# Strided attention on one core: own semaphores, whole-block casts in turn, and two streams that begin at a 128-instruction border

## The chip, the cores and the metric

The kernel runs on one core of a Trainium2 chip. The metric is device time in microseconds; three runs of the kernel before took 129.59, 129.45 and 129.51 us, median 129.51.

The core has five engines with an instruction stream each: PE (TensorE, matrix products), DVE (VectorE), ACT (ScalarE), POOL (GpSimd) and SP (SyncE, which here issues all transfers). Sixteen DMA engines move data between HBM and SBUF.

## The reference

Q, K and V are 8 x 12 x 1024 x 64 in float32. Every query attends to 16 keys, those at positions 0, 64, 128, ... of its head:

```python
attend_positions = np.arange(0, seq, stride)          # stride 64: 16 positions
q, k, v = Q[:, :, i:i+1, :], K[:, :, attend_positions, :], V[:, :, attend_positions, :]
scores  = einsum('bhqd,bhkd->bhqk', q, k) / sqrt(dim)
weights = exp(scores - max(scores)); weights /= sum(weights) + 1e-10
result[:, :, i, :] = einsum('bhqk,bhkd->bhqd', weights, v)
```

All of Q (25 MB) is read and as much output is written; of K and V only 0.4 MB each is needed.

## The kernel before

The 96 heads are worked on in 24 blocks of four heads (`g`, 0 to 23); a block has 1 MB of queries and 1 MB of output. Each block goes through these steps, named by function:

- `load(g)`: SP issues one transfer of the block's queries into one of ten float32 buffers `qn`.
- `cast(g)`: float32 to bf16 into `qb` (two buffers), the first half on POOL (L200) and the second on ACT (L201), 1,024 columns each.
- `transpose(g)`: DVE transposes 32 x 32 tiles of 32-bit pairs into `qt` (L205, two buffers).
- `scores(g)`: PE makes the scores with four matrix products from `k_t` and `qt` (L212); ACT takes the exponential of each half into `w` (L223).
- `values(g)`: POOL spreads the block's value rows over a mask into `v` (L191, three buffers). Four columns more of `v` hold a selector, so that the product also gives the sums of the weights.
- `outputs(g, c)`, c = 0, 1, 2: PE multiplies `w` by `v` for 3, 2 and 3 query groups (L237, two PSUM buffers in turn); DVE takes the reciprocal of the sums (L245); for c = 0 and 1 DVE multiplies into `out_sb` (L247), for c = 2 ACT copies the sums out of PSUM (L249) and POOL multiplies in place (L250).
- `store(g)`: SP issues one transfer of `out_sb` (eight buffers) to HBM.

Ahead of the loop POOL builds an identity matrix and from it `perm_v` with eight copies (L118), POOL and DVE clear `k_t` and the `w` buffers (L123, L127, L129), and DVE builds the selector `s_sel` from two iotas in three steps (L132 to L139), three copies of it and a mask. `key_rows` and `keys` lay out the keys in thirds: the first ahead of the loop, the others within blocks 1 to 3 and 5 to 7; `value_rows` does the values in halves, the second within block 4.

The order of work on every engine is the order in which the code records it (`manual_schedule`). In round `g` the code records `transpose(g + 2)`, `scores(g + 1)`, `values(g + 2)`, `cast(g + 3)`, then the three `outputs` of block g, then `store(g)` and `load(g + 10)`. Buffers come from rotating pools, and the framework places the semaphores and the waits. Its transfers go round eight semaphores, so that each transfer waits until the eighth one before it has landed.

Of the kernel before, what the change touches and what calls it, by code (L numbers as in the profile page):

```python
# [11 lines left out]
FP32 = mybir.dt.float32  # L12
BF16 = mybir.dt.bfloat16
# [29 lines left out]

@with_exitstack  # L50
def kernel(
# [24 lines left out]
    const = ctx.enter_context(tc.tile_pool(name="const", bufs=1))  # L76
    qn_pool = ctx.enter_context(tc.tile_pool(name="qn", bufs=QBUFS))
    out_pool = ctx.enter_context(tc.tile_pool(name="outsb", bufs=OBUFS))
    qb_pool = ctx.enter_context(tc.tile_pool(name="qb", bufs=2))
    qt_pool = ctx.enter_context(tc.tile_pool(name="qt", bufs=2))  # L80
    rec_pool = ctx.enter_context(tc.tile_pool(name="rec", bufs=2))
    psum_sc = ctx.enter_context(tc.tile_pool(name="psc", bufs=2, space=bass.MemoryType.PSUM))
    psum_o = ctx.enter_context(tc.tile_pool(name="po", bufs=2, space=bass.MemoryType.PSUM))

    ctx.enter_context(tc.manual_schedule())


    k_raw = const.tile([P, NC, D], FP32, name="k_raw")
    v_raw = const.tile([P, NC, D], FP32, name="v_raw")
    kv_src = [[stride * D, P], [2 * HG * SD, NC], [1, D]]  # L90
    qn = {}

    def load(g):
        qn[g] = qn_pool.tile([P, 32 * D], FP32, name="qn", tag="qn")
        n = P if g < 2 else 32
        _copy(nc, qn[g], _ap_with(Q, [[HG * SD // n, n], [1, HG * SD // n]], g * HG * SD))

    nc.sync.dma_start(k_raw, _ap_with(K, kv_src))
    load(0)
    nc.sync.dma_start(v_raw, _ap_with(V, kv_src))  # L100
# [3 lines left out]

    identity = const.tile([P, P], BF16, name="identity")
    make_identity(nc, identity)
    id_v = identity.rearrange("p (c b a k) -> p c b a k", c=2, b=2, a=2)

    perm_v = const.tile([P, 2, 2, 2, 2, NK], BF16, name="perm_v")

    iota_p = const.tile([P, 1], I16, name="iota_p")
    nc.gpsimd.iota(iota_p, pattern=[[0, 1]], base=0, channel_multiplier=1)
    col4 = const.tile([P, 4], I16, name="col4")
    nc.gpsimd.iota(col4, pattern=[[1, 4]], base=0, channel_multiplier=0)
    for c in range(2):
        for a in range(2):
            for e in range(2):
                nc.gpsimd.tensor_copy(  # L118
                    out=perm_v[:, c, a, :, e], in_=id_v[:, c, :, a]
                )  # L120

    k_t = const.tile([P, NG, 2, KW], BF16, name="k_t")
    nc.vector.memset(k_t[:, 0:8], 0.0)  # L123
    w_bufs = []
    for i in range(3):
        w = const.tile([P, 8, P], BF16, name=f"w{i}")
        nc.vector.memset(w, 0.0)  # L127
        w_bufs.append(w)
    nc.gpsimd.memset(k_t[:, 8:NG], 0.0)  # L129

    slot_i = const.tile([P, 1], I16, name="slot_i")
    nc.vector.tensor_scalar(  # L132
        out=slot_i, in0=iota_p, scalar1=4, scalar2=3,
        op0=ALU.logical_shift_right, op1=ALU.bitwise_and,
    )
    slot_f = const.tile([P, 1], FP32, name="slot_f")
    nc.vector.tensor_copy(out=slot_f, in_=slot_i)
    s_sel = const.tile([P, 4], BF16, name="s_sel")
    nc.vector.tensor_scalar(  # L139
        out=s_sel, in0=col4, scalar1=slot_f, scalar2=None, op0=ALU.is_equal  # L140
    )
    v_bufs = []
    for i in range(3):
        v = const.tile([P, 4 * D + 4], BF16, name=f"v{i}")
        nc.vector.tensor_copy(out=v[:, 4 * D :], in_=s_sel)
        v_bufs.append(v)
    mask = const.tile([P, 4, D], BF16, name="mask")
    nc.vector.tensor_copy(out=mask, in_=s_sel.unsqueeze(2).to_broadcast([P, 4, D]))

    k_bf = const.tile([P, NC, D], BF16, name="k_bf")  # L150
    k_r = const.tile([P, NC, D], BF16, name="k_r")
    v_bf = const.tile([P, NC, D], BF16, name="v_bf")
    v_rep = const.tile([P, NC, 2, D], BF16, name="v_rep")


    def key_rows(m):
        part = slice(4 * m, 4 * m + 4)
        nc.scalar.copy(k_bf[:, part], k_raw[:, part])  # L158
        nc.vector.transpose(  # L159
            k_r[:, part].rearrange("p n d -> p (n d)").bitcast(I32),  # L160
            k_bf[:, part].rearrange("p n d -> p (n d)").bitcast(I32),
        )


    def keys(m, c):
        for s in range(4):
            src, dst, col = 32 * (2 * c + s % 2), 32 * (2 * (s % 2) + s // 2), NK + 32 * s
            op = nc.vector.tensor_copy if m == 0 and s >= 2 else nc.scalar.copy
            op(  # L169
                k_t[dst : dst + 32, 8 * m + c : 8 * m + 8 : 2, :, col : col + NK],  # L170
                k_r[src : src + 32, 4 * m : 4 * m + 4].rearrange(
                    "p n (a k f) -> p a n f k", a=2, f=2
                )[:, s // 2],
            )


    def value_rows(n):
        for c in range(2):
            vp = psum_sc.tile([P, NC // 2, D], FP32, name="vp", tag="sc")
            nc.tensor.matmul(  # L180
                vp, lhsT=perm_v[:, c].rearrange("p a b e k -> p (a b e k)"),
                rhs=v_bf[:, 6 * n : 6 * n + 6], start=True, stop=True,
            )
            nc.vector.tensor_copy(out=v_rep[:, 6 * n : 6 * n + 6, c], in_=vp)  # L184

    qb, qt, wt, vb, rec, out_sb = {}, {}, {}, {}, {}, {}


    def values(g):
        vb[g] = v_bufs[g % 3]  # L190
        nc.gpsimd.tensor_tensor(  # L191
            out=vb[g][:, 0 : 4 * D].rearrange("p (s d) -> p s d", s=4), in0=mask,
            in1=v_rep[:, g // 2, g % 2].unsqueeze(1).to_broadcast([P, 4, D]),
            op=ALU.mult,
        )

    def cast(g):
        qb[g] = qb_pool.tile([P, 32 * D], BF16, name="qb", tag="qb")
        half = 16 * D
        nc.gpsimd.tensor_copy(out=qb[g][:, 0:half], in_=qn[g][:, 0:half])  # L200
        nc.scalar.copy(qb[g][:, half:], qn[g][:, half:])  # L201

    def transpose(g):
        qt[g] = qt_pool.tile([P, 32 * D], BF16, name="qt", tag="qt")
        nc.vector.transpose(qt[g].bitcast(I32), qb[g].bitcast(I32))  # L205

    def scores(g):
        sc = psum_sc.tile([P, 512], FP32, name="sc", tag="sc")
        q = qt[g]
        for e in range(2):  # L210
            for f in range(2):
                nc.tensor.matmul(  # L212
                    sc, lhsT=k_t[:, g, f, NK * (1 - e) : NK * (1 - e) + P],
                    rhs=_ap_with(
                        q, [q.ap[0], [D, 8], [16 * D, 2], [2, 32]],
                        extra_offset=8 * D * e + f,
                    ),
                    start=e + f == 0, stop=e + f == 2,
                )
        w = wt[g] = w_bufs[g % 3]  # L220
        for a in range(2):
            wa = w[64 * a : 64 * a + 64]
            nc.scalar.activation(  # L223
                out=_ap_with(wa, [wa.ap[0], [P, 8], [1, 2], [2, 32]], extra_offset=64 * a),
                in_=sc[64 * a : 64 * a + 64].rearrange("p (t x q) -> p t x q", t=8, x=2),
                func=AF.Exp, bias=0.0, scale=scale,
            )


    def outputs(g, c):  # L230
        if c == 0:
            out_sb[g] = out_pool.tile([P, 4, 8, D], FP32, name="out_sb", tag="out_sb")
            rec[g] = rec_pool.tile([P, 8, 4], FP32, name="rec", tag="rec")
        i0, n = ((0, 3), (3, 2), (5, 3))[c]
        ps = psum_o.tile([P, 3, 512], FP32, name="o_ps", tag="o")
        for i in range(n):
            nc.tensor.matmul(  # L237
                ps[:, i, 0 : 4 * D + 4], lhsT=wt[g][:, i0 + i], rhs=vb[g],
                start=True, stop=True,
            )  # L240
        r = rec[g][:, i0 : i0 + n]
        o = ps[:, 0:n, 0 : 4 * D].rearrange("p i (s d) -> p i s d", s=4)
        to = out_sb[g][:, :, i0 : i0 + n].rearrange("p s i d -> p i s d")
        by = r.unsqueeze(3).to_broadcast([P, n, 4, D])
        nc.vector.reciprocal(r, ps[:, 0:n, 4 * D : 4 * D + 4])  # L245
        if c < 2:
            nc.vector.tensor_tensor(out=to, in0=o, in1=by, op=ALU.mult)  # L247
        else:
            nc.scalar.copy(to, o)  # L249
            nc.gpsimd.tensor_tensor(out=to, in0=to, in1=by, op=ALU.mult)  # L250

    def store(g):
        o = out_sb[g]
        _copy(
# [3 lines left out]
        )  # L258
# [8 lines left out]
    nc.vector.tensor_copy(out=v_bf, in_=v_raw)  # L267
# [16 lines left out]
    for g in range(NG):  # L284
# [13 lines left out]
        if g + QBUFS < NG:  # L298
            load(g + QBUFS)
# [33 lines left out]
```

## Time and profile before

| What | Value |
|---|---|
| median of three runs | 129.51 us (129.45 to 129.59) |
| profiled execution: span | 127.7 us (the page gives no other time of it) |
| median less that span | 1.8 us |
| busy share of the span | DVE 69%, ACT 67%, POOL 63%, PE 50% |
| data queue (q1) | 51.12 MB, 96.7% of 16 DMA engines |
| mean rate | 401 GB/s over the span |
| HBM | 25.95 MB read, 25.17 MB written |

The span runs from the first to the last instruction of the profiled execution. Idle time of an engine in the page is put down to whatever ended it. The DMA share of a stretch is the mean over the 16 DMA engines of the time that their packets took, so it can pass 1 a little where packets overlap. The granted clock is the share of full speed at which PE ran; it was 0.858 over the span.

### The profile page before, as it was taken

The page shows a single profiled execution, that of the slowest core. Times are in us where ns is not written, and L with a number is a line of the kernel's source. Part 1 is how long each engine was busy: PE and PEld are TensorE (multiplying, and loading weights), DVE is VectorE, ACT ScalarE, POOL GpSimd, SP SyncE. Part 2 cuts the span into 40 slices and gives each one's busy share as a digit, 9 for nine tenths or more (in the row PEclk, how much of TensorE's full clock was granted, in tenths as well). Part 3 has the DMA queues.
Part 4 walks back from the last instruction along what each step waited for, and adds up shares of the span by engine and source line. Part 5 has one row for each costly group of instructions (what it writes and reads, how often), then busy time and mean ns, then how long its engine had stood idle before and what let it go on. Part 6 is the DMA issues. An engine that isn't in the chain of part 4 may idle for free.

```text
span 127.7 us, 1234 instructions
## 1 busy us (share of the span) xinstructions
PE 63.5 (50%) x292; PEld 29.8 (23%) x292; DVE 88.5 (69%) x167; ACT 86.1 (67%) x120; POOL 80.1 (63%) x89
## 2 busy tenths in 40 slices
PE   0006559256756628653696646366777646410000
PEld 0002223123322313332243313133423313200000
DVE  6956691869698696859769799797987976720000
ACT  4161917886999968999958979979787885320000
POOL 8933709554875876577866997969689694450000
PEclk9999999996799986999559999999856999955555
DMA  2999989998997998989989999999999999999980
GB/s 66 379 320 467 472 349 482 380 452 354 467 482 326 498 413 369 495 362 421 493 357 431 470 380 444 434 403 462 428 393 449 398 428 418 428 426 421 431 352 36
DMA packets 7911, 51.20 MB, mean 401 GB/s; under 512 B 3872, under 2 KB 3872, under 8 KB 3872
## 3 DMA queue, kind: packets, MB, share of 16 engines
q1 hardware_dynamic: 7904, 51.12, 96.7%
q8 instruction: 2, 0.03, 0.1%
q14 instruction: 5, 0.04, 0.1%
HBM read 25.95 MB, written 25.17 MB: 400 GB/s over the span
## 4 chain that ended last, share of the span: by engine, by line
POOL 37%; issue 33%; DVE 10%; PE 6%; ACT 2%; POOLq 1%; DVEq 0%
POOL qb L200 15%; POOL out_sb L250 12%; POOL v L191 10%; PE sc L212 4%; DVE out_sb L247 3%; PE o_ps L237 2%; DVE s_sel L139 2%; POOLq L328 1%; DVE w L127 1%; DVE qt L205 1%; ACT qb L201 1%; DVE rec L245 1%; DVE k_t L123 1%; ACT out_sb L249 1%; ACT k_t L169 0%
## 5 line engine op out<-in xcount | busy, mean ns | idle before, releaser
L237 PE MATMUL o_ps<-v,w 128*128 128x260 bf16 x192 | 37.9, 316 | 37.3 <-DVE out_sb L247 33.2
L250 POOL TENSOR_TENSOR out_sb<-out_sb,rec 128x768 f32<-128x768 f32 x24 | 35.3, 1472 | 29.2 <-ACT out_sb L249 29.2
L247 DVE TENSOR_TENSOR out_sb<-o_ps,rec 128x768 f32<-128x768 f32 (+1 forms) x48 | 39.6, 825 | 1.6
L223 ACT ACTIVATE w<-sc 64x512 bf16<-64x512 f32 x48 | 35.3, 736 | 5.0 <-PE sc L212 4.6
L205 DVE STREAM_TRANSPOSE qt<-qb 128x1024 int32<-128x1024 int32 x24 | 29.5, 1230 | 11.1 <-ACT qb L201 7.1
L212 PE MATMUL sc<-qt,k_t 128*128 128x512 bf16 x96 | 31.7, 463 | 10.4 <-DVE qt L205 10.4
L237 PEld LDWEIGHTS <-w 128*128 128x128 bf16 x192 | 18.6, 108 | 60.5 <-DVE out_sb L247 41.6
L249 ACT COPY out_sb<-o_ps 128x768 f32<-128x768 f32 x24 | 19.2, 800 | 15.8 <-DVE rec L245 15.5
L200 POOL CAST qb<-qn 128x1024 bf16<-128x1024 f32 x24 | 25.0, 1040 | 4.1 <-DMA qn<-in_Q_dram 4.1
L201 ACT CAST qb<-qn 128x1024 bf16<-128x1024 f32 x24 | 25.0, 1047 | 0.7
L245 DVE RECIPROCAL rec<-o_ps 128x12 f32<-128x12 f32 (+1 forms) x72 | 15.1, 210 | 5.6 <-PE o_ps L237 5.2
L191 POOL TENSOR_TENSOR v<-mask,v_rep 128x256 bf16<-128x256 bf16 x24 | 16.1, 670 | 1.0 <-DVE v_rep L184 1.0
L212 PEld LDWEIGHTS <-k_t 128*128 128x128 bf16 x96 | 10.7, 111 | 21.1 <-ACT k_t L169 8.0
L169 ACT COPY k_t<-k_r 32x128 bf16<-32x128 bf16 x20 | 5.9, 296 | 2.3 <-DVE k_r L159 2.0
L129 POOL MEMSET k_t<- 128x4608 bf16 x1 | 3.9, 3937 | 0.0
L184 DVE CAST v_rep<-vp 128x384 bf16<-128x384 f32 x4 | 2.2, 542 | 1.9 <-PE vp L180 1.8
L158 ACT CAST k_bf<-k_raw 128x256 bf16<-128x256 f32 x3 | 1.2, 408 | 2.9 <-DMA k_raw<-in_K_dram 2.9
L139 DVE TENSOR_SCALAR s_sel<-col,slot_f 128x4 bf16<-128x4 int16 x1 | 2.6, 2553 | 0.1
L159 DVE STREAM_TRANSPOSE k_r<-k_bf 128x128 int32<-128x128 int32 x3 | 0.9, 309 | 2.3 <-ACT k_bf L158 2.3
L180 PE MATMUL vp<-v_bf,perm_v 128*128 128x384 bf16 x4 | 1.6, 412 | 1.1 <-DVE v_rep L184 0.6
L158 ACT ACT_TABLE_LOAD x1 | 1.3, 1283 | 0.7 <-PEq L314 0.7
L123 DVE MEMSET k_t<- 128x1152 uint32 x1 | 1.0, 1018 | 1.0 <-PEq L314 1.0
(17 smaller groups left out, 6.6 us busy)
## 6 DMA issues: line engine op xcount, KB each, us to landing
qn<-in_Q_dram SPq DMA_DIRECT2D x24, 1024.0 KB, 16.0
out_dram<-out_sb SPq DMA_DIRECT2D x24, 1024.0 KB, 14.8
k_raw<-in_K_dram SPq DMA_DIRECT2D x1, 384.0 KB, 4.2
v_raw<-in_V_dram SPq DMA_DIRECT2D x1, 384.0 KB, 7.2
```

Of the source, the lines that this page charges most:

```text
L169: op(k_t[dst : dst + 32, 8 * m + c : 8 * m + 8 : 2, :, col : col + NK], k_r[src : src + 32, 4 * m : 4 * m + 4].rearrange("p n (a k f) -> p ...
L191: nc.gpsimd.tensor_tensor(out=vb[g][:, 0 : 4 * D].rearrange("p (s d) -> p s d", s=4), in0=mask, in1=v_rep[:, g // 2, g % 2].unsqueeze(1).t ...
L200: nc.gpsimd.tensor_copy(out=qb[g][:, 0:half], in_=qn[g][:, 0:half])
L201: nc.scalar.copy(qb[g][:, half:], qn[g][:, half:])
L205: nc.vector.transpose(qt[g].bitcast(I32), qb[g].bitcast(I32))
L212: nc.tensor.matmul(sc, lhsT=k_t[:, g, f, NK * (1 - e) : NK * (1 - e) + P], rhs=_ap_with(q, [q.ap[0], [D, 8], [16 * D, 2], [2, 32]], extra_ ...
L223: nc.scalar.activation(out=_ap_with(wa, [wa.ap[0], [P, 8], [1, 2], [2, 32]], extra_offset=64 * a), in_=sc[64 * a : 64 * a + 64].rearrange( ...
L237: nc.tensor.matmul(ps[:, i, 0 : 4 * D + 4], lhsT=wt[g][:, i0 + i], rhs=vb[g], start=True, stop=True,)
L245: nc.vector.reciprocal(r, ps[:, 0:n, 4 * D : 4 * D + 4])
L247: nc.vector.tensor_tensor(out=to, in0=o, in1=by, op=ALU.mult)
L249: nc.scalar.copy(to, o)
L250: nc.gpsimd.tensor_tensor(out=to, in0=to, in1=by, op=ALU.mult)
```

## The change

Four things are done in one edit.

1. A small class, `Program`, records every operation with what it reads and writes. `plan` works out which earlier operations each must wait for, drops waits that others imply, and `emit` issues all streams inside one `tile_critical` block with a semaphore of its own for each engine and for each transfer buffer. Tiles are allocated once; nothing rotates.
2. Casts from block 4 on are not split: even blocks are cast whole on ACT, odd blocks whole on POOL.
3. `values(g)` on POOL waits for `store(g - 8)`, so that the writers of the output buffer need no such wait. The limit of eight transfers in flight is gone.
4. Before their streams, ACT and POOL have an alignment directive: the next instruction lies at a border of 128 instructions; the padding is jumped over.

The setup is shorter too: one iota and two DVE steps for the selector, one copy for the three selector columns, one memset for the three `w` buffers, four copies for `perm_v`.

```diff
--- before.py
+++ after.py
+class Program:
+    ENGINES = ("PE", "DVE", "ACT", "POOL", "SP")
+    def __init__(self, nc, tc):
+        self.nc, self.tc, self.ops = nc, tc, []
+        self.writer, self.readers = {}, {}
+
+    def op(self, engine, fn, reads=(), writes=(), after=(), lane=None):
+        i = len(self.ops)
+        deps, own = set(after), set()
...
+        self.ops.append(dict(engine=engine, fn=fn, lane=lane or engine, deps=deps, own=own))
+        return i
+
+    def plan(self):
...
+            for d in sorted(o["deps"], reverse=True):
+                p = self.ops[d]
+                if p["lane"] == e and (e == "PE" or d not in o["own"]):
+                    continue
+                if known[e].get(p["lane"], -1) >= d:
+                    continue
+                waits.append(d)
...
+    def emit(self):
...
+        counts = self.plan()
+        sems = {lane: self.tc.alloc_semaphore(f"at_{lane}") for lane in counts}
+        with self.tc.tile_critical(no_gpsimd_drain=True):
+            for e in ("ACT", "POOL"):
+                engines[e].addr_align(128, max_nops=0)
+            for o in self.ops:
+                for d in o["waits"]:
+                    p = self.ops[d]
+                    engines[o["engine"]].wait_ge(sems[p["lane"]], p["count"])
+                r = o["fn"]()
+                if o["step"]:
+                    r.then_inc(sems[o["lane"]], o["step"])
+            for lane, n in counts.items():
+                if lane.startswith("out"):
+                    nc.sync.wait_ge(sems[lane], n)
...
-    iota_p = const.tile([P, 1], I16, name="iota_p")
-    nc.gpsimd.iota(iota_p, pattern=[[0, 1]], base=0, channel_multiplier=1)
-    col4 = const.tile([P, 4], I16, name="col4")
-    nc.gpsimd.iota(col4, pattern=[[1, 4]], base=0, channel_multiplier=0)
+    op("POOL", lambda: nc.gpsimd.iota(ahead4, pattern=[[-16, 4]], base=64, channel_multiplier=1),
+       writes=["ahead4"])
     for c in range(2):
         for a in range(2):
-            for e in range(2):
-                nc.gpsimd.tensor_copy(
-                    out=perm_v[:, c, a, :, e], in_=id_v[:, c, :, a]
-                )
+            op("POOL", lambda c=c, a=a: nc.gpsimd.tensor_copy(
+                out=perm_v[:, c, a],
+                in_=id_v[:, c, :, a].unsqueeze(2).to_broadcast([P, 2, 2, NK]),
+            ), reads=["identity"], writes=[f"perm{c}{a}"])
...
+    op("DVE", lambda: nc.vector.memset(w_all, 0.0),
+       writes=[f"w{i}{a}" for i in range(3) for a in range(2)])
...
+    op("DVE", lambda: nc.vector.tensor_single_scalar(
+        out=slot4, in_=ahead4, scalar=48, op=ALU.bitwise_and
+    ), reads=["ahead4"], writes=["slot4"])
+    op("DVE", lambda: nc.vector.tensor_single_scalar(
+        out=s_sel, in_=slot4, scalar=0, op=ALU.is_equal
+    ), reads=["slot4"], writes=["s_sel"])
...
     def values(g):
-        vb[g] = v_bufs[g % 3]
-        nc.gpsimd.tensor_tensor(
+        v = v_bufs[g % 3]
+        op("POOL", lambda: nc.gpsimd.tensor_tensor(
...
+        ), reads=["mask", f"v_rep{g // 12}{g % 2}"], writes=[f"v{g % 3}"],
+           after=[stored[g - OBUFS]] if g >= OBUFS else [])
...
     def cast(g):
-        qb[g] = qb_pool.tile([P, 32 * D], BF16, name="qb", tag="qb")
-        half = 16 * D
-        nc.gpsimd.tensor_copy(out=qb[g][:, 0:half], in_=qn[g][:, 0:half])
-        nc.scalar.copy(qb[g][:, half:], qn[g][:, half:])
+        q, b = qn[g % QBUFS], qb[g % 2]
+        if g >= 4:
+            e, fn = ("POOL", nc.gpsimd.tensor_copy) if g % 2 else ("ACT", nc.scalar.copy)
+            op(e, lambda: fn(b, q), reads=[f"qn{g % QBUFS}"], writes=[f"qb{g % 2}0", f"qb{g % 2}1"])
+            return
+        op("POOL", lambda: nc.gpsimd.tensor_copy(out=b[:, 0:half], in_=q[:, 0:half]),
+           reads=[f"qn{g % QBUFS}"], writes=[f"qb{g % 2}0"])
+        op("ACT", lambda: nc.scalar.copy(b[:, half:], q[:, half:]),
+           reads=[f"qn{g % QBUFS}"], writes=[f"qb{g % 2}1"])
...
+    prog.emit()
```

The order in which the code records the blocks' steps is unchanged, and so is what each other step computes.

More of the change, by code (lines that the diff above doesn't have):

```diff
@@ L74 @@
     OBUFS = 8
[L76 to L82, printed above, removed]
@@ new lines @@
+    qt = [sb.tile([P, 32 * D], BF16, name=f"qt{i}") for i in range(2)]
+    rec = [sb.tile([P, 8, 4], FP32, name=f"rec{i}") for i in range(2)]
+    w_all = sb.tile([P, 3, 8, P], BF16, name="w_all")
+    v_all = sb.tile([P, 3, 4 * D + 4], BF16, name="v_all")
+    w_bufs, v_bufs = [w_all[:, i] for i in range(3)], [v_all[:, i] for i in range(3)]
+    k_t = sb.tile([P, NG, 2, KW], BF16, name="k_t")
+    k_bf = sb.tile([P, NC, D], BF16, name="k_bf")
+    k_r = sb.tile([P, NC, D], BF16, name="k_r")
+    v_bf = sb.tile([P, NC, D], BF16, name="v_bf")
@@ new lines @@
+    v_rep = sb.tile([P, NC, 2, D], BF16, name="v_rep")
+    identity = sb.tile([P, P], BF16, name="identity")
+    perm_v = sb.tile([P, 2, 2, 2, 2, NK], BF16, name="perm_v")
+    ahead4 = sb.tile([P, 4], I16, name="ahead4")
+    slot4 = sb.tile([P, 4], I16, name="slot4")
+    s_sel = sb.tile([P, 4], BF16, name="s_sel")
+    mask = sb.tile([P, 4, D], BF16, name="mask")
+    sc_ps = [ps.tile([P, 512], FP32, name=f"sc{i}") for i in range(2)]
+    o_ps = [ps.tile([P, 3, 512], FP32, name=f"o{i}") for i in range(2)]
@@ L129 @@
[L129 to L141, printed above, removed]
@@ new lines @@
+    op("DVE", lambda: nc.vector.memset(k_t[:, 0:8], 0.0),
+       writes=[f"k_t0{c}{s}" for c in range(2) for s in range(4)])
+    op("DVE", lambda: nc.vector.memset(w_all, 0.0),
+       writes=[f"w{i}{a}" for i in range(3) for a in range(2)])
+    op("POOL", lambda: nc.gpsimd.memset(k_t[:, 8:NG], 0.0),
+       writes=[f"k_t{m}{c}{s}" for m in (1, 2) for c in range(2) for s in range(4)])
+    op("DVE", lambda: nc.vector.tensor_single_scalar(
+        out=slot4, in_=ahead4, scalar=48, op=ALU.bitwise_and
+    ), reads=["ahead4"], writes=["slot4"])
@@ L156, in key_rows @@
+    op("DVE", lambda: nc.vector.tensor_single_scalar(
+        out=s_sel, in_=slot4, scalar=0, op=ALU.is_equal
+    ), reads=["slot4"], writes=["s_sel"])
+    op("DVE", lambda: nc.vector.tensor_copy(
+        out=v_all[:, :, 4 * D :], in_=s_sel.unsqueeze(1).to_broadcast([P, 3, 4])
+    ), reads=["s_sel"], writes=["vs"])
+    op("DVE", lambda: nc.vector.tensor_copy(
+        out=mask, in_=s_sel.unsqueeze(2).to_broadcast([P, 4, D])
+    ), reads=["s_sel"], writes=["mask"])
     def key_rows(m):
         part = slice(4 * m, 4 * m + 4)
-        nc.scalar.copy(k_bf[:, part], k_raw[:, part])
@@ L159, in key_rows @@
-        nc.vector.transpose(
+        op("ACT", lambda: nc.scalar.copy(k_bf[:, part], k_raw[:, part]),
+           reads=["k_raw"], writes=[f"k_bf{m}"])
+        op("DVE", lambda: nc.vector.transpose(
             k_r[:, part].rearrange("p n d -> p (n d)").bitcast(I32),
             k_bf[:, part].rearrange("p n d -> p (n d)").bitcast(I32),
-        )
+        ), reads=[f"k_bf{m}"], writes=[f"k_r{m}"])
     def keys(m, c):
@@ L181, in value_rows @@
                 vp, lhsT=perm_v[:, c].rearrange("p a b e k -> p (a b e k)"),
                 rhs=v_bf[:, 6 * n : 6 * n + 6], start=True, stop=True,
-            )
-            nc.vector.tensor_copy(out=v_rep[:, 6 * n : 6 * n + 6, c], in_=vp)
-    qb, qt, wt, vb, rec, out_sb = {}, {}, {}, {}, {}, {}
+            ), reads=["v_bf"] + [f"perm{c}{a}" for a in range(2)],
+               writes=[f"sc{b}0", f"sc{b}1"])
+            op("DVE", lambda vp=vp, c=c: nc.vector.tensor_copy(
+                out=v_rep[:, 6 * n : 6 * n + 6, c], in_=vp
+            ), reads=[f"sc{b}0", f"sc{b}1"], writes=[f"v_rep{n}{c}"])
@@ L236, in outputs @@
+        o_buf, o_key, to_key = o_ps[t], f"o{t}", f"out{g % OBUFS}{c}"
+        w, v, slot = w_bufs[g % 3], v_bufs[g % 3], out_sb[g % OBUFS]
         for i in range(n):
[L237 to L243, printed above, removed]
+            op("PE", lambda i=i: nc.tensor.matmul(
+                o_buf[:, i, 0 : 4 * D + 4], lhsT=w[:, i0 + i], rhs=v, start=True, stop=True,
+            ), reads=[f"w{g % 3}0", f"w{g % 3}1", f"v{g % 3}", "vs"], writes=[o_key])
@@ L257, in store @@
             _ap_with(o, [o.ap[0], [1, 1], [1, 32 * D]]),
-        )
+        ), reads=[f"out{g % OBUFS}{c}" for c in range(3)], lane=f"out{g % OBUFS}")
     key_rows(0)
@@ L266 @@
     cast(1)
-    nc.vector.tensor_copy(out=v_bf, in_=v_raw)
+    op("DVE", lambda: nc.vector.tensor_copy(out=v_bf, in_=v_raw), reads=["v_raw"], writes=["v_bf"])
     value_rows(0)
```

161 lines of the change are left out of this document (102 added, 59 removed).

## The prediction

> **What bounds the kernel now.** I read the page's queue table first.
>
> ```profile
> span 127.7 us, 1234 instructions
> ...
> q1 hardware_dynamic: 7904, 51.12, 96.7%
> q8 instruction: 2, 0.03, 0.1%
> q14 instruction: 5, 0.04, 0.1%
> ```
>
> The data queue holds the 16 DMA engines for 96.7% of the span, while no compute engine passes 69%. The seven small instruction packets matter further down. Next, the end of the span by windows (columns: PE, PEld, DVE, ACT, POOL busy, then granted clock, DMA share, GB/s):
>
> ```profile
> 115.00:120.00 5.00, 0.00 (x0) 0.00 (x0) 0.00 (x0) 0.00 (x0) 0.00 (x0) 0.50 1.02 428
> 122.00:123.00 1.00, 0.00 (x0) 0.00 (x0) 0.00 (x0) 0.00 (x0) 0.00 (x0) 0.50 0.95 401
> 124.00:125.00 1.00, 0.00 (x0) 0.00 (x0) 0.00 (x0) 0.00 (x0) 0.00 (x0) 0.50 0.31 131
> 125.00:126.00 1.00, 0.00 (x0) 0.00 (x0) 0.00 (x0) 0.00 (x0) 0.00 (x0) 0.50 0.12 49
> ```
>
> Compute is over at 115, and the DMA still has stores to move. From 15 us on its share reads 0.99 to 1.02 in every window, so the queues never run dry. At the end it does not stop at once: after 124 only a few engines still work. The trace's landing records say the same. The first query loads land over their 16 engines within 0.7 us; the last store's parts land from 123.97 to 126.83, a spread of 2.9 us. That spread grows in steps of about 0.7 us, just after the instruction packets at 39.5, 47.0, 47.6, 57.5, 89.3, 99.0 and 106.6 us: an 8,192-byte fetch holds its engine 0.31 us, and the data packet behind it runs about 0.36 us long. The span ends 0.89 us after the last landing.
>
> So the bound is the most delayed DMA engine. Compute has a margin: the last store is issued at 115.01 us. How long does a lone store need? k_raw takes 4.2 us from issue to its last landing; its 96 packets of 19 ns per engine are 1.8 us, a store's 8 packets of 311 ns are 2.5 us, so 4.2 + 0.7 = 4.9. A last store issued at 122.0 would still land at 126.8: the margin is 7 us. The chain that ended last shows what paces compute:
>
> ```profile
> POOL 37%; issue 33%; DVE 10%; PE 6%; ACT 2%; POOLq 1%; DVEq 0%
> ```
>
> In the timeline of two blocks it is a loop:
>
> ```profile
> 73.32 1.47 POOL L250 TENSOR_TENSOR out_sb<-out_sb,rec 128x768 f32<-128x768 f32 x1 [0.19 <-ACT out_sb L249]
> 74.75 0.67 POOL L191 TENSOR_TENSOR v<-mask,v_rep 128x256 bf16<-128x256 bf16 x1
> 75.36 1.04 POOL L200 CAST qb<-qn 128x1024 bf16<-128x1024 f32 x1
> 76.44 1.25 DVE L205 STREAM_TRANSPOSE qt<-qb 128x1024 int32<-128x1024 int32 x1
> ...
> 79.55 0.22 DVE L245 RECIPROCAL rec<-o_ps 128x12 f32<-128x12 f32 x1
> 79.81 0.80 ACT L249 COPY out_sb<-o_ps 128x768 f32<-128x768 f32 x1
> 80.69 1.47 POOL L250 TENSOR_TENSOR out_sb<-out_sb,rec 128x768 f32<-128x768 f32 x1 [0.20 <-ACT out_sb L249]
> ```
>
> GpSimd's multiply, values, cast, then VectorE's transpose and five more instructions, ScalarE's copy, GpSimd's multiply again: 73.32 to 80.69, 7.37 us for two blocks, 3.68 a block. The DMA needs 4.9 us for a block's load and store (2 x 1.22 and 8 x 0.311), so compute runs ahead while loads are issued, but not when only ten stores (2.45 us each) remain.
>
> **The casts in turn (from block 4).** Each odd block's cast is now one GpSimd instruction of 2,048 columns, and it lies in that loop. Its length, from these rows:
>
> ```profile
> L201 ACT CAST qb<-qn 128x1024 bf16<-128x1024 f32 x24 | 25.0, 1047 | 0.7
> L200 POOL CAST qb<-qn 128x1024 bf16<-128x1024 f32 x24 | 25.0, 1040 | 4.1 <-DMA qn<-in_Q_dram 4.1
> L118 POOL COPY perm_v<-identity 128x32 bf16<-128x32 bf16 x8 | 1.3, 210 | 0.0
> L158 ACT CAST k_bf<-k_raw 128x256 bf16<-128x256 f32 x3 | 1.2, 408 | 2.9 <-DMA k_raw<-in_K_dram 2.9
> ```
>
> On GpSimd (1040 - 210) / 992 = 0.84 ns a column, on ScalarE (1047 - 408) / 768 = 0.83. So a whole cast is 1.04 + 0.85 = 1.89 us on either engine; strict doubling, 2.08, is the upper end. The loop grows to 7.37 + 0.85 = 8.22 us, 4.11 a block. The ten odd casts 5 to 23 lie in ten such loops; I count nine, because the blocks around the first take 4.5 us or more, held by the key copies. That is 9 x 0.85 = 7.65 us later for the last store. (With 2.08: 9.4.) The even blocks' casts sit on ScalarE, 0.85 longer every second block; its two blocks sum to 4 x 0.74 + 1.90 + 2 x 0.80 = 6.5 us of 8.2, so that costs nothing while GpSimd's loop is the longer.
>
> PE's clock enters the loop too: in the half-clock stretch the two blocks whose stores are issued at 93.63 and 101.69 took 8.06 us. Before pays about 2 us for such stretches. With PE stretched over more time there may be fewer of them; bounds 0 and 2 us less. I take 1.
>
> **Start.** DVE's L139 (128x4) takes 2.55 us and ends at 6.56, when GpSimd's 3.94 us memset L129 ends (6.55); k_r, k_t and ScalarE's first cast wait behind it. [...] The new L227/L230 pair will be held as well, but the memset starts earlier: one iota of 0.08 less, and four copies for eight (8 x 0.15 against 4 x 0.18), 0.56 in all. ScalarE's first cast then waits for its load alone, 0.38 earlier. The new entry into the critical block costs one hand-off by semaphore and branch: the barrier rows put that at 0.08 to 0.16 us; I take 0.15, on the first DMA too. Net for compute: 0.25 earlier.
>
> **Semaphores.** GpSimd and ScalarE lose 39 waiting instructions each in the built program, DVE 26; those rows are 17 to 38 ns and run beside the engine's previous instruction, so nothing is counted (bounds 0 and 1 us over the run). Before, a transfer waits for the eighth one before it (SP waits 10.8 + 9.0 us so); the DMA was at 1.00 meanwhile, so dropping that gains nothing. The added wait: `values` waits on GpSimd for store g-8, with cast and multiply behind it. That store was issued some six blocks, 24 us, earlier and the median landing takes 14.8, so it is covered; beyond 24 it would stop compute.
>
> **Fetches.** The built streams shrink: ScalarE 169 to 125, GpSimd 146 to 97, DVE 218 to 191, SP 103 to 75 instructions; PE stays (617, 619). [...] DVE had executed 63 and 196 instructions at the packets of 39.5 and 106.6, about 128 apart: with 191 in all the second falls away. The most delayed engine took that last step, 0.75 us. I take this one step; the bounds are none and all three of its steps, 2.2 us.
>
> **Sum.** DMA side: 126.83 + 0.15 - 0.75 = 126.2 for the last landing. Compute side: 115.0 + 7.65 - 1 - 0.25 = 121.4 for the last issue, + 4.9 = 126.3. They meet; I take 126.2. The exit adds a hand-off, 0.2 (0.1 to 0.4): span 126.2 + 0.89 + 0.2 = 127.3, 0.4 under the profiled 127.7. The profiled execution has its span alone on the page; the median 129.51 lies 1.8 above it, so 129.1.
>
> **Rivals.** *The cast loop outlasts the DMA (slower).* If the half-clock stretches stay, the last store goes out at 122.4 and lands at 127.3; with 2.08 us casts, at 129.1. With 0.89, 0.2 and 1.8 added: 130.2, up to 132.0. It decides once the last store is issued after 122.0. For it: the loop is exact in the trace, the margin is as large as the loss. Against it: DMA delay on the other side, PE's lower load.
>
> *The fetches are not what delays the last engine, or the border does not remove them.* Then 126.83 + 0.15 + 1.1 + 1.8 = 129.9, slower by 0.3%. The steps in landing speak against it. [...]
>
> *More is gained:* all three steps of the last engine go and PE stays at full clock: the last store is issued at 120.4 and lands at 125.4, which gives 128.3.
>
> *The two cancel:* last landing 126.6, about 129.5.
>
> **Numbers.** Forecast 0.35, more gained 0.15, cancel 0.12, cast loop 0.28, fetches 0.10. A difference below 0.2%, 0.26 us, counts as no change. Faster 0.50, same 0.12, slower 0.38. The range runs from the larger gain, 128.3, to the cast loop with half of the doubled casts' extra, 131.1; the forecast's own case is 128.8 to 129.25.
>
> **What would show it.** GpSimd's cast near 1.89 us; odd loops of 8.2 us; the last store issued between 120.5 and 122.4; two or three instruction packets fewer; DMA share 1.00 until about 120 and then small gaps. A last issue after 122.5, or DMA share below 0.9 before 118, makes the forecast wrong, and so does an unchanged number of instruction packets.

## The result: slower by 1.1%

The changed kernel took 131.0 us (median of 4, 130.15 to 131.79), the kernel before beside it 129.55; the ratio is 1.0114, 95% interval 1.0089 to 1.0139. Forecast were 129.1 us and faster. The first rival, the cast loop that outlasts the DMA, is what happened, at a price inside its range. Ratios leave out executions in a slower state; only `before_border_third` had any, five of its twelve.

### The profile after

The page's queue rows and its chain that ended last:

```profile
span 130.0 us, 1078 instructions
...
q1 hardware_dynamic: 7904, 51.12, 95.1%
q8 instruction: 2, 0.03, 0.1%
q14 instruction: 3, 0.02, 0.1%
...
DVE 30%; ACT 27%; PE 18%; POOL 16%; issue 4%; DVEq 0%; SPq 0%
```

Two instruction packets fewer, as forecast, but a span 2.3 us longer. The chain names four engines where POOL stood alone before. The windows at the end (PE, PEld, DVE, ACT, POOL busy, then granted clock, DMA share, GB/s):

```profile
110.00:115.00 5.00, 2.29 (x12) 0.97 (x10) 3.33 (x6) 2.27 (x4) 3.33 (x3) 0.89 1.02 429
115.00:118.00 3.00, 2.21 (x8) 0.90 (x6) 1.15 (x3) 1.99 (x3) 1.47 (x1) 0.62 0.68 287
118.00:120.00 2.00, 1.11 (x7) 0.52 (x8) 1.47 (x6) 0.80 (x1) 0.07 (x1) 1.00 0.96 397
120.00:122.00 2.00, 1.13 (x5) 0.29 (x4) 1.74 (x4) 0.11 (x1) 1.40 (x1) 0.68 0.34 139
122.00:124.00 2.00, 0.00 (x0) 0.00 (x0) 0.00 (x0) 0.69 (x1) 1.23 (x1) 0.50 0.78 324
```

From 115 us on the DMA waits for compute: 0.68, then 0.34, where before stood at 1.02 with all engines done. The last store is issued at 124.27 (before 115.01) and its last part lands at 128.49; 1.50 us of exit follow. The casts took what was forecast (busy us, mean ns of one):

```profile
L292 ACT CAST qb<-qn 128x2048 bf16<-128x2048 f32 x10 | 19.0, 1898 | 0.2
L292 POOL CAST qb<-qn 128x2048 bf16<-128x2048 f32 x10 | 18.9, 1889 | 0.0
```

What was not forecast stands in the chain of waits, here four blocks of it, from one ACT copy to the same one four blocks on (start, us, what):

```profile
87.70 1.90 ACT qb L292
89.60 0.03 issue
89.62 0.81 ACT out_sb L346
90.43 0.07 issue
90.50 1.47 POOL out_sb L347
91.97 0.63 POOL v_all L279
92.60 1.84 POOL qb L292
94.47 1.25 DVE qt L300
...
97.71 1.71 PE sc L308 x4
...
104.53 1.90 ACT qb L292
106.43 0.03 issue
106.46 0.81 ACT out_sb L346
```

89.62 to 106.46 is 16.84 us for four blocks, 8.42 for two; the forecast was 8.22, from 7.37 before. (From block 9 to block 21 two blocks take 8.37 on average; before they took 7.66 there, so 7.37 was its loop where PE had its full clock.) ACT's whole cast is on the chain, directly ahead of ACT's copy, which POOL's multiply waits for; so are PE's four score matmuls, at half clock: 1.71 us, where the kernel before shows 1.06 at full clock.

Earlier, where ACT also copies the keys (L253), its whole cast is on the chain with no work of PE near it. From ACT's copy for block 2 on:

```profile
31.11 0.80 ACT out_sb L346
31.91 0.19 ACT k_t L253
...
33.04 0.73 ACT w_all L319
33.78 0.73 ACT w_all L319
...
34.54 1.91 ACT qb L292
36.47 1.25 DVE qt L300
```

That is the cast of block 6; those of blocks 8 and 10, at 43.99 and 54.19 us, stand in the chain as well.

### The profile page after: what moved, and what is told of

Read it like the earlier page. It is cut to its first block, busy times and chain, and to the rows that moved or that the text cites. A ratio compares the mean times of both kernels' runs of the same rounds, so it can differ in the third digit from the quotient of the medians.

```text
span 130.0 us, 1078 instructions
## 1 busy us (share of the span) xinstructions
PE 68.0 (52%) x292; PEld 30.3 (23%) x292; DVE 90.5 (70%) x162; ACT 84.5 (65%) x110; POOL 78.0 (60%) x74
## 4 chain that ended last, share of the span: by engine, by line
DVE 30%; ACT 27%; PE 18%; POOL 16%; issue 4%; DVEq 0%; SPq 0%
DVE out_sb L343 12%; DVE qt L300 9%; PE sc L308 9%; ACT qb L292 9%; PE o L332 8%; ACT w_all L319 8%; ACT out_sb L346 7%; POOL out_sb L347 7%; POOL qb L292 6%; DVE rec L340 4%; POOL v_all L279 2%; DVE slot L227 2%; ACT qb L296 2%; ACT k_t L253 1%; DVE w_all L222 1%
## 5 line engine op out<-in xcount | busy, mean ns | idle before, releaser
L332 PE MATMUL o<-v_all,w_all 128*128 128x260 bf16 x192 | 39.2, 328 | 41.4 <-DVE out_sb L343 35.9
L319 ACT ACTIVATE w_all<-sc 64x512 bf16<-64x512 f32 x48 | 35.2, 734 | 8.8 <-PE sc L308 8.4
L343 DVE TENSOR_TENSOR out_sb<-o,rec 128x768 f32<-128x768 f32 (+1 forms) x48 | 39.6, 824 | 1.6
L300 DVE STREAM_TRANSPOSE qt<-qb 128x1024 int32<-128x1024 int32 x24 | 29.6, 1235 | 15.3 <-POOL qb L292 8.0
L346 ACT COPY out_sb<-o 128x768 f32<-128x768 f32 x24 | 19.2, 798 | 22.8 <-DVE rec L340 22.6
L332 PEld LDWEIGHTS o<-v_all,w_all 128*128 128x128 bf16 x192 | 18.5, 113 | 65.0 <-DVE out_sb L343 44.2
L292 ACT CAST qb<-qn 128x2048 bf16<-128x2048 f32 x10 | 19.0, 1898 | 0.2
L292 POOL CAST qb<-qn 128x2048 bf16<-128x2048 f32 x10 | 18.9, 1889 | 0.0
L279 POOL TENSOR_TENSOR v_all<-mask,v_rep 128x256 bf16<-128x256 bf16 x24 | 16.0, 668 | 1.7 <-DVE v_rep L273 1.7
L253 ACT COPY k_t<-k_r 32x128 bf16<-32x128 bf16 x20 | 5.9, 295 | 2.5 <-DVE k_r L244 2.2
L294 POOL CAST qb<-qn 128x1024 bf16<-128x1024 f32 x4 | 4.2, 1047 | 4.0 <-DMA qn<-in_Q_dram 4.0
L296 ACT CAST qb<-qn 128x1024 bf16<-128x1024 f32 x4 | 4.1, 1043 | 0.1
```

The source lines that it names most:

```text
L253: op(e, lambda fn=fn, s=s, src=src, dst=dst, col=col: fn(k_t[dst : dst + 32, 8 * m + c : 8 * m + 8 : 2, :, col : col + NK], k_r[src : src ...
L279: op("POOL", lambda: nc.gpsimd.tensor_tensor(out=v[:, 0 : 4 * D].rearrange("p (s d) -> p s d", s=4), in0=mask, in1=v_rep[:, g // 2, g % 2] ...
L292: op(e, lambda: fn(b, q), reads=[f"qn{g % QBUFS}"], writes=[f"qb{g % 2}0", f"qb{g % 2}1"])
L296: op("ACT", lambda: nc.scalar.copy(b[:, half:], q[:, half:]), reads=[f"qn{g % QBUFS}"], writes=[f"qb{g % 2}1"])
L300: op("DVE", lambda: nc.vector.transpose(qt[g % 2].bitcast(I32), qb[g % 2].bitcast(I32)), reads=[f"qb{g % 2}0", f"qb{g % 2}1"], writes=[f"q ...
L319: op("ACT", lambda a=a, wa=wa: nc.scalar.activation(out=_ap_with(wa, [wa.ap[0], [P, 8], [1, 2], [2, 32]], extra_offset=64 * a), in_=sc[64 ...
```

## The experiments

Medians and ratios are against the kernel before, run beside them. "Last store" is the issue of block 23's store in the profiled execution.

### Which part of the change costs: the casts

**`halved`:** the changed kernel, all casts halved.

```diff
-        if g >= 4:
+        if g >= 400:
```

> The changed kernel with every cast halved between GpSimd and ScalarE, as before; everything else of the change stays. Theory (the whole casts on both engines lengthen one loop, and that loop outlasts the DMA): the last store is issued at 115 to 116 us instead of 124.3, the DMA share stays at 1.00 to the end, the last landing comes at 126.83 + 0.24 (later first DMA) - 0.75 (no fetch step on the last engine) = 126.3, the exit takes the 1.49 us of the changed kernel, span 127.8, time 129.6: no difference from before. Rival (the kernel's own semaphores, the hand-offs or the new order cost the time): the last store stays after 120 and the time at 130.5 or more.

**`act_whole`, `pool_whole`:** whole casts on one engine only.

```diff
-        if g >= 4:
+        if g >= 4 and g % 2 == 0:    # act_whole; == 1: pool_whole
```

> The changed kernel with only the even casts from block 4 whole (ScalarE); the odd ones are halved again. Theory (the two engines' whole casts cost together: ScalarE's holds up its own copy, which GpSimd's multiply waits for, GpSimd's holds up the transpose): laid out in stream order with the rows' durations, one engine's alone brings the last store to 116 to 119 us, still inside the DMA's margin; last landing 126.3, time 129.6. Rival (GpSimd's cast alone is to blame and ScalarE's costs nothing, as the prediction had it): last store 115 to 116, and the two-block loop is 7.4 us as before.

> The changed kernel with only the odd casts from block 5 whole (GpSimd); the even ones are halved again. Theory (both engines' casts together): last store 118 to 120 us, two-block loop 8.2 us, last landing 126.3, time 129.6. Rival (GpSimd's cast alone is to blame): last store 123 or later, DMA share below 0.9 before 121, time 130.5 or more.

**`before_whole`:** the kernel before with whole casts and nothing else.

```diff
     def cast(g):
         qb[g] = qb_pool.tile([P, 32 * D], BF16, name="qb", tag="qb")
         half = 16 * D
+        if g >= 4:
+            (nc.gpsimd.tensor_copy if g % 2 else nc.scalar.copy)(out=qb[g], in_=qn[g])
+            return
```

> The kernel before with nothing changed but the casts: whole from block 4, even on ScalarE, odd on GpSimd. Theory (the whole casts are the cause): the last store is issued some 9 us later, at 124, lands 4.3 later at 128.3, exit 0.89 as before, span 129.2, time 131.0. Rival (semaphores, hand-offs or order are the cause): time within 0.3 us of before, 129.5.

| Kernel | Median, us | Ratio (95%) | Last store | Last landing |
|---|---|---|---|---|
| `halved` | 129.83 | 1.0037 (1.0019 to 1.0055) | 118.96 | 126.37 |
| `act_whole` | 130.01 | 1.0046 (1.0031 to 1.0061) | 119.72 | 126.21 |
| `pool_whole` | 130.06 | 1.0048 (1.0032 to 1.0064) | 120.92 | 126.44 |
| changed kernel | 131.0 | 1.0114 (1.0089 to 1.0139) | 124.27 | 128.49 |
| `before_whole` | 131.23 | 1.0130 (1.0089 to 1.0172) | 124.99 | 129.21 |

The whole casts alone, on the kernel before, give a loss as large as the whole change; without them the rest of the change is slower by only 0.4%. While the last store is issued before about 121 the last landing does not move: the DMA sets the end. The expected last stores were missed, by 3 us in `halved` and by 0.7 and 0.9 in `act_whole` and `pool_whole`; the three times came 0.2 to 0.5 us above the expected 129.6. `before_whole` came within 0.3 us of its expected time. In `halved` POOL waited in the added wait of `values` (waited for: us in total, times, longest):

```profile
POOL v_all L279 <- DMA out_dram<-out_sb: 2.4, 2, 1.8
```

The prediction held that this wait is covered by 24 us of lead. It is not once compute runs ahead of the DMA; it cost no time there, because the DMA was at about 1.00 until 124:

```profile
115.00:118.00 3.00, 0.90 (x4) 0.28 (x3) 1.43 (x4) 0.80 (x1) 1.48 (x2) 0.50 1.00 421
118.00:120.00 2.00, 0.00 (x0) 0.00 (x0) 0.00 (x0) 0.00 (x0) 0.93 (x1) 0.50 1.03 434
120.00:122.00 2.00, 0.00 (x0) 0.00 (x0) 0.00 (x0) 0.00 (x0) 0.00 (x0) 0.50 0.99 418
122.00:124.00 2.00, 0.00 (x0) 0.00 (x0) 0.00 (x0) 0.00 (x0) 0.00 (x0) 0.50 1.03 434
```

Because of that wait, and of a half clock in its last block (0.50 from 115 us on), the last store of `halved` is not the compute time to compare with. The start of POOL's multiply shows the casts' cost better (us; the wait first comes at 99 us):

| Kernel | block 0 | block 8 | block 16 | block 23 |
|---|---|---|---|---|
| before | 19.41 | 58.18 | 88.05 | 113.51 |
| `halved` | 20.00 | 58.51 | 89.33 | 117.46 |
| `act_whole` | 19.70 | 60.70 | 92.02 | 118.22 |
| `pool_whole` | 19.71 | 58.28 | 91.53 | 119.42 |
| changed kernel | 19.69 | 60.88 | 94.39 | 122.77 |
| `after_again` (the changed kernel once more) | 19.74 | 60.47 | 94.56 | 121.14 |
| `busy4` (see below) | 19.70 | 59.63 | 93.57 | 119.85 |

Counted from block 0 to block 8, ACT's whole casts cost 2.5 us against `halved` (those of blocks 6, 8 and 10, about 0.83 each), POOL's nothing. To block 16 ACT's cost 3.0, POOL's 2.5, and both together 5.4 to 5.5: their sum.

### Is it the cast's place in the loop?

**`third`:** whole casts, three `qb` buffers, each cast issued a block further ahead.

```diff
-    qb = [... for i in range(2)]
+    qb = [... for i in range(3)]          # and qb[g % 3] throughout
     transpose(1)
     cast(2)
+    cast(3)
...
-        if g + 3 < NG:
-            cast(g + 3)
+        if g + 4 < NG:
+            cast(g + 4)
```

> The changed kernel with whole casts, but three cast buffers instead of two and each cast issued one block further ahead (block g+4 instead of g+3). Theory (the casts cost because they lie between the multiply and the transpose of the next blocks; with a block more of lead they leave the loop): the two-block loop falls from 8.4 us to about 7.2, the last store is issued at 113.5 to 117, DMA share 1.00 to the end, last landing 126.3, span 127.85, time 129.8. Rival (the casts' engine time or the clock of PE sets the pace, wherever the cast stands): last store after 121, 130.5 or more.

Measured: 129.9 us, ratio 1.0044 (1.0027 to 1.0062), last store 115.89, last landing 126.42. The group row of DVE's transpose, first of the changed kernel, then of `third` (busy, mean ns | idle before it and what ended it):

```profile
L300 DVE STREAM_TRANSPOSE qt<-qb 128x1024 int32<-128x1024 int32 x24 | 29.6, 1235 | 15.3 <-POOL qb L292 8.0 <-ACT qb L292 3.6 <-ACT qb L296 3.5
```

```profile
L300 DVE STREAM_TRANSPOSE qt<-qb 128x1024 int32<-128x1024 int32 x24 | 28.7, 1197 | 0.8 <-ACT qb L296 0.4 <-PE sc L308 0.4
```

The same casts of the same length no longer delay the transpose (15.3 us of waiting became 0.8), and 8.4 us of the last store's 9.3 us of delay are gone. With the granted clock as it was (0.82 over the span, the changed kernel 0.83), that is the cast's place and not its engine time.

**`before_third`, `before_border_third`:** the same on the kernel before (there `tile_pool(name="qb", bufs=3)`), without and with the border.

> The kernel before with whole casts from block 4, three cast buffers and each cast one block further ahead; no semaphores of its own, no border. Theory (a cast with a block more of lead leaves the loop): last store at 113.5 to 117, against 124.99 for whole casts with two buffers; the DMA sets the end, last landing 126.5 to 126.9, exit 0.89, time 129.3 (within 0.2% of before). Rival (whole casts cost wherever they stand): 130.5 or more.

> The same with the border for ScalarE and GpSimd at the start: GpSimd's stream of 116 instructions and its end fit one 128-instruction block, ScalarE's crosses once. Theory (the DMA sets the end, shorter streams fetch less while it is full): two 8 KB packets fewer than the five of before, spread of the last landings about 2.2 us, last landing 126.2, time 129.0, faster by 0.3%. Rival (fetches that leave the busy time come back at the start, or do not hit the engine that ends last): 129.35, no change.

Measured: ratio 1.0000 (0.9981 to 1.0019), median 129.38; and 1.0032 (1.0002 to 1.0062). The first is no different from before. Its profiled execution, at 130.41 the longest of its twelve, had its last store at 123.56, outside the expected range. From 61 to 100 us, first of before, then of this execution (third from the end the clock):

```profile
61.00:100.00 39.00, 25.91 (x125) 12.66 (x124) 33.54 (x61) 32.92 (x41) 31.08 (x31) 0.83 1.01 427
```

```profile
61.00:100.00 39.00, 26.46 (x94) 11.40 (x95) 25.79 (x46) 24.01 (x27) 24.39 (x21) 0.59 1.01 429
```

In that stretch its chain that ended last has no cast in it; it goes through PE and DVE, at 0.59 of full clock. So a cast that is out of the way does not by itself bring an early last store. Why the clock was so low in this execution stays open. The second was to be 0.3% faster and was not. Neither beats the kernel before.

### Which way does PE's load move its clock?

The prediction took 1 us off for fewer half-clock stretches, because the same matmuls lie in more time.

**`light_pe`:** two of four score matmuls left out.

```diff
-            for f in range(2):
+            for f in range(2 if g < 4 else 1):
...
-                    start=e + f == 0, stop=e + f == 2,
+                    start=e + f == 0, stop=e == 1 and f == (1 if g < 4 else 0),
```

> The changed kernel with two of the four matmuls of scores left out from block 4 on (the terms with f = 1), so the scores are not the reference's; it is there for the time of the loop only. Laid out in stream order with the rows' durations, PE's shorter work leaves the two-block loop at full clock at 8.2 us, as with four matmuls, but takes the half-clock stretches out of it (four matmuls at half clock take 1.9 us, two 1.0). Theory (the half-clock stretches lengthen a loop that now holds both casts and PE's scores): last store at 119.5 to 121.5 instead of 124.3, inside the DMA's margin, time 129.8. Rival (the casts alone make the excess over the prediction's 121.4): last store at 123.5 or later, time 130.5 or more.

**`busy4`, `busy2`:** matmuls added where PE is idle.

```diff
+    def keep_busy(g):
+        s = (sc_turn[0] + 1) % 2
+        for i in range(4):               # busy2: range(2)
+            op("PE", lambda: nc.tensor.matmul(
+                sc_ps[s], lhsT=k_t[:, 0, 0, 0:P],
+                rhs=k_t[:, 0:2].rearrange("p g f w -> p (g f w)")[:, 0:512],
+                start=True, stop=True,
+            ), reads=[...], writes=[f"sc{s}0", f"sc{s}1"])
+
     def outputs(g, c):
+        if c == 2 and 4 <= g < NG - 2:
+            keep_busy(g)
```

> The changed kernel with four matmuls more per block (72 in all, 512 columns, into the scores bank that is free, result unused) on PE ahead of the last third of outputs in blocks 4 to 21, where PE idles for DVE. At full clock they take 0.9 us of that idle time. Theory A (PE drops to half clock where it idles, so the slower loop with its longer waits brings more half-clock stretches): the granted clock rises from 0.83 to 0.95 or more, the two-block loop stays at 8.0 to 8.2 us, last store at 119.5 to 121.5, inside the DMA's margin, last landing 126.3, time 129.8. Theory B (the prediction's: PE's load brings the half-clock stretches): the clock falls below 0.83, the loop grows, last store at 124.5 or later, time 131 or more.

> The same with two matmuls more per block (36 in all). Theory A: clock between the changed kernel's 0.83 and that of four matmuls more, last store between 120.5 and 123.5, time 129.8 to 130.8. Theory B: clock below 0.83, last store at 124 or later, time 131 or more.

**`after_again`:** the changed kernel once more.

> The changed kernel itself once more, beside the others on one chip. Both theories: last store issued at 123 to 125, landing 4.2 later, time 130.6 to 131.2. Against the same kernel without the border (130.43): if the border's jump at the start delays compute, this one is 0.3 to 0.5 slower; if not, the two agree within 0.2.

| Kernel | Median, us | Ratio (95%) | Last store | Granted clock, median of the runs |
|---|---|---|---|---|
| `light_pe` | 130.26 | 1.0059 (1.0036 to 1.0082) | 121.77 | 0.67 |
| `after_again` | 130.98 | 1.0107 (1.0070 to 1.0144) | 122.63 | 0.83 |
| `busy2` | 129.70 | 1.0034 (1.0010 to 1.0059) | 122.19 | 0.87 |
| `busy4` | 129.59 | 1.0024 (1.0009 to 1.0040) | 121.34 | 0.90 |

The last store of `after_again` came 0.4 us before its expected range, that of `light_pe` 0.3 after; `busy4` and `busy2` stayed in theirs. The clock over the span rises with the work given to PE; the kernel before, run beside them on both chips, stood at 0.84. The page's clock rows (40 slices, tenths of full speed), first of `light_pe`, then of `busy4`:

```profile
PEclk9999999965775569555955558997556995559555
```

```profile
PEclk9999999965899999995999599997799999999555
```

The same in one stretch, 48 to 112 us (PE busy first, third from the end the clock), of `light_pe`, the changed kernel, `busy2` and `busy4`:

```profile
48.00:112.00 64.00, 35.70 (x150) 15.36 (x150) 49.92 (x92) 48.23 (x60) 46.07 (x39) 0.68 1.01 426
```

```profile
48.00:112.00 64.00, 39.76 (x180) 18.58 (x180) 49.53 (x91) 49.09 (x61) 45.52 (x39) 0.81 1.01 426
```

```profile
48.00:112.00 64.00, 41.20 (x206) 19.11 (x210) 49.52 (x92) 48.49 (x60) 46.06 (x39) 0.95 1.01 425
```

```profile
48.00:112.00 64.00, 48.72 (x235) 22.79 (x240) 49.27 (x91) 48.68 (x60) 45.73 (x38) 0.92 1.00 424
```

So in these runs it is less work on PE that brings more half clock (0.67, 0.83, 0.87 and 0.90 over the span for ever more matmuls), the opposite of what the prediction assumed. It is not a matter of the amount alone: in this stretch `busy2` stood above `busy4` (0.95 against 0.92), and one profile of each cannot tell why. The expected 0.95 for `busy4` was not reached. 72 matmuls whose result nobody uses make the changed kernel 1.4 us faster (131.0 to 129.59; the intervals of `busy4` and `after_again` do not overlap).

Where the clock costs is not the steady loop. From block 9 to block 21 two blocks take 8.37 us in the changed kernel, 8.32 in `busy4` and 8.30 in `light_pe`. The time lies ahead of block 8 (41.19 us from block 0, against 39.93 in `busy4`) and in the last two blocks (7.17 us from block 21 to 23 against 5.73; the clock from 115 to 118 us was 0.62). In `after_again` the two are 40.73 and 5.90.

With PE's short scores the loop of `light_pe` does not feel the clock. POOL's multiplies, every second one:

```profile
72.72 1.47 POOL L347 TENSOR_TENSOR out_sb<-out_sb,rec 128x768 f32<-128x768 f32 x1 [2.40 <-ACT out_sb L346]
...
80.93 1.47 POOL L347 TENSOR_TENSOR out_sb<-out_sb,rec 128x768 f32<-128x768 f32 x1 [2.22 <-ACT out_sb L346]
...
89.14 1.47 POOL L347 TENSOR_TENSOR out_sb<-out_sb,rec 128x768 f32<-128x768 f32 x1 [2.22 <-ACT out_sb L346]
```

72.72 to 80.93 to 89.14: 8.21 us each time, against the forecast's 8.22. ACT's casts are then off the chain. The forecast's loop was right for a loop without PE's clock. Its median missed the expected 129.8 all the same: its spans run from 127.9, the profiled one, to 128.7.

### The border and the fetches

**`noborder`, `halved_noborder`:** the two lines of the alignment directive taken out of the changed kernel and of `halved`. **`before_border`:** the directive put ahead of the kernel before.

```diff
-            for e in ("ACT", "POOL"):
-                engines[e].addr_align(128, max_nops=0)
```

> The changed kernel without the border: ScalarE and GpSimd begin their streams where they fall. Theory (the cast loop sets the end, so what delays a single DMA engine is hidden): the instruction packets in the busy time come back, two or three more than the changed kernel's three after 40 us, the last store is issued at 123.5 to 124.5 and the time stays at 131.0. Rival (the border's jump at the start delays compute, ScalarE's table load 0.6 us later than before): everything 0.3 earlier, 130.7.

> The changed kernel with all casts halved and without the border. Theory (fetches delay the most loaded DMA engine, and here the DMA sets the end): against the same kernel with the border two or three more instruction packets, the spread of the last store's landings grows from 1.83 to about 2.6 us, the last landing comes 0.7 later, at 127.1, time 130.5. Rival (the fetches do not set the end): last landing 126.4 and 129.8, as with the border.

> The kernel before with nothing changed but the border for ScalarE and GpSimd at its start. Their streams are 160 and 127 instructions long, so each still crosses a border, but ScalarE once and GpSimd only near its end. Theory (the fetches set the last landing): two of the five 8 KB packets leave the busy time, last landing 126.1 to 126.5, the exit stays at 0.89, time 128.9, faster by 0.4%. Rival (the border buys nothing): last landing 126.8, 129.4.

| Kernel | Median, us | Ratio (95%) | Last landing | Spread of the last store's landings |
|---|---|---|---|---|
| `noborder` | 130.43 | 1.0086 (1.0054 to 1.0118) | 127.51 | 0.19 |
| `halved_noborder` | 129.72 | 1.0023 (1.0010 to 1.0036) | 126.51 | 2.20 |
| `halved` | 129.83 | 1.0037 (1.0019 to 1.0055) | 126.37 | 1.83 |
| `before_border` | 129.33 | 0.9995 (0.9979 to 1.0012) | 126.70 | 2.68 |
| before | 129.51 | 1 | 126.83 | 2.86 |

Between `halved_noborder` and `halved` the border takes packets out of the busy time: those of q14 stand at 44.2, 47.6 and 58.9 us without it, one, at 44.5, with it. But the last landing moves by 0.14 us, not by the 0.7 expected, and the median does not gain. In `before_border` the two packets that were to leave the busy time did not: five stand between 40.4 and 119.9 us, as many as before. That run shows what the directive costs there (nothing), not what fewer packets would bring. With the border two packets are fetched at 1.8 to 2.3 us, when the first transfers start. That in `halved` the first landing of block 0's load is at 7.28 us, in `halved_noborder` at 7.08 and in before at 6.80, fits fetches that were moved rather than removed, but no run separates it. Whether the border costs the changed kernel 0.5 us, as `noborder` suggests, stays open; the intervals overlap, and its last store at 123.30 was 0.2 us ahead of the range that its theory gave.

For the time the border bought nothing: `halved` with it is no faster (1.0037) than without it (1.0023), and `before_border` is no different from before (0.9995).

## Why the prediction was wrong

| Step | Predicted | Measured |
|---|---|---|
| whole cast | 1.89 us | 1.89 (POOL), 1.90 (ACT) |
| two-block loop | 8.22 us | 8.37 on average over blocks 9 to 21; 8.21 at best in `light_pe` |
| ready output of block 0 | 0.25 earlier | 0.28 later |
| block 0 to block 23: casts and clock | +7.65 - 1 = +6.65 | +8.98; +7.29 in `after_again` |
| of it, block 0 to block 8 | +2.55 (three casts) | +2.42; +1.96 |
| of it, block 8 to block 23 | +5.10 - 1 = +4.10 | +6.56; +5.33 |
| last store issued | 121.4 | 124.27; 122.63 in `after_again` |
| issue to last landing | 4.9 | 4.22 |
| DMA side, last landing | 126.2 | 126.2 to 126.4 in `halved`, `act_whole`, `pool_whole` |
| exit | +0.2 | +0.6 |
| span | 127.3 | 130.0; median of the runs 129.2 |

Two steps failed: the last store at 121.4, which put compute inside the DMA's margin (1 to 3), and the gain on the DMA's side, which the later exit took back (4 to 6).

1. **The term of the sum that failed is the -1 us for fewer half-clock stretches.** Its reason pointed the wrong way: with two of four score matmuls left out PE's granted clock fell to 0.67 (`light_pe`), and in the changed kernel's runs it did not rise (0.82 and 0.83; before 0.84). Against the casts' 7.65 the -1 came out as +1.33 and -0.36 in the two profiles of the kernel. With matmuls added, `busy4` came out at -1.60 and issued its last store at 121.34, where the forecast had 121.4.
2. **ScalarE's even casts were put at nothing, and that was wrong.** The 6.5 us for ScalarE's two blocks left out its key copies. A block with a whole cast and four of them holds ScalarE for 1.90 + 4 x 0.295 + 2 x 0.74 + 0.80 = 5.4 us. From block 2 to block 3 the changed kernel took 5.35 us, before 4.50. The sum did not show it, by luck: up to block 8 the forecast had 2.55 us for POOL's casts of blocks 7, 9 and 11, which cost nothing in `pool_whole`; in `act_whole` ACT's cost 2.5.
3. **The edge was right, partly by luck.** A lone store needs 4.22 us (also in `before_whole` and `noborder`), so the end begins to move when the last store is issued after 126.3 - 4.2 = 122.1 us; the rival said 122.0, with a store 0.7 us too long and an end of the DMA 0.5 too late. The forecast sat 0.7 us short of that edge; the two profiles of the kernel lie 0.5 and 2.2 us beyond it, and its runs reach from 130.15 to 131.88. In both profiles the time is the issue of the last store and 7.5 us, so the median of 131.0 means a last store near 123.5 (an estimate): 2.1 us after the forecast, of which 0.5 are the start.
4. **The exit and the start cost the gain of the DMA side.** The last landing of `halved` is 0.46 us earlier than before, but the barrier at the end of the critical block takes 0.53 us in the instruction records and the exit 1.50 against 0.89. The first transfer is issued 0.23 us later (0.96 against 0.73). The later exit (0.61) less the earlier landing makes the span of `halved` 0.15 us longer than before's, and 0.2 us more lie outside the span (below). So even with casts that cost nothing the change is slower by 0.4% (`halved`, `third`): "faster" was out of reach.
5. **The shorter setup gained nothing:** ACT, DVE and POOL first wait for the critical block's entry, and ACT's first instruction comes at 1.32 us against 0.73.

```profile
ACT L242 <- SPq L114: 1.3, 1, 1.3
DVE k_t L220 <- SPq L114: 1.3, 1, 1.3
POOL ahead L205 <- SPq L114: 1.0, 1, 1.0
```

6. **The fetch step was half right.** With fewer packets the spread of the last landings did shrink (2.86 to 1.83 us in `halved`; 2.20 without the border), and the DMA-side sum met the measured landing. But the border's part of the earlier landing is 0.14 us, and most of the 0.46 came without it. In before the spread grew at three of the places named, near 39.5, 47 and 106.6 us; after the packets at 57.5, 89.3 and 99.0 it stayed within 0.1. Reading a step in the spread as time gained was too simple, since the least delayed engine became later too (first part of the last store: 123.97 before, 124.54 in `halved`, of which 0.23 is the later start).

## What to carry to other kernels

A step that moves within a margin still has to be priced with every engine in the loop, and in every stretch: ScalarE's longer casts cost little where GpSimd's loop was the longer (0.5 us from block 8 to block 16 in `act_whole`, against `halved`), and about 0.83 us each where ScalarE also copied keys. Before counting on a faster clock for PE, look at what it does in the time added: here the clock fell from 0.83 to 0.67 as PE's work was taken away, and unused matmuls in the idle time gave back 1.4 us. A cast that must be long belongs a buffer further ahead; here that took away 8.4 of 9.3 us of delay, though no kernel with it was faster than the one before.

## What the runs showed of the hardware that was not expected

- Granted clock over the span against work, one kernel: 0.67, 0.83, 0.87, 0.90 as 40 matmuls were left out, none changed, 36 and 72 added. Fewer matmuls, a lower clock.
- The time outside the span is not one constant. Median of time less span: 1.77 us for before, 1.80 for the changed kernel, 1.99 for `halved` (1.86 to 2.13 over its runs), 2.17 for `pool_whole` (2.11 to 2.22), but 1.81 for `halved_noborder` and 1.77 for `third`. `halved` shows instruction packets at 127.9 and 129.6 us, about and after its end; `pool_whole` shows none, so what makes the difference stays open.
